# A scan one chunk ahead, a late operand, two gather buffers: one change to a layer with 32 experts on one core

## The chip, the cores and the metric

The kernel runs on one core of one Trainium2 chip. The metric is device time in microseconds, of one launch that computes the whole layer. The core has a matrix engine (PE, with its weight loads shown apart as PEld), a vector engine (DVE), an activation engine (ACT), GpSimd (POOL), a sync engine (SP) that mostly starts transfers, and 16 DMA engines. Each engine works through its own list of instructions in order and waits on semaphores.

## What is computed

The reference is one layer with 1024 tokens of width 1024, in float32:

```python
# mixing: three head groups side by side, then one output projection
h = rms_norm(x, norm_mix_g) * (1 + scale1) + shift1
p = h @ w_in                          # split into the inputs of the three groups
y = concat(ssd_mixer(...),            # 512 wide: scan over chunks of 128 tokens
           forgetting_attention(...), # 256 wide
           conformer_conv(...))       # 256 wide
x = x + gate * (y @ w_out)
# experts: 4 groups of 8, top-1 group, top-2 experts in it
h = rms_norm(x) * (1 + scale2) + shift2
weights = top_p / sum(top_p) * p_group
x = x + gate2 * sum_k weights_k * expert_k(h)
expert(h) = (silu(h @ w_gate) * (h @ w_up)) @ w_down      # 1024 -> 512 -> 1024, 32 experts
out = rms_norm(x) * g
```

(The block is shortened; names of small parameters are left out.) The scan of one chunk needs the state that the chunk before it left.

## The kernel before

The 1024 tokens lie in 8 blocks of 128. Float32 products are made of three matmuls: each operand is split into a high part, which ACT casts, and a low part, which DVE or POOL subtracts (the helper `split`, lines 127 and 128), and high by high, low by high and high by low are added in PSUM.

The kernel is written against a planner. It takes every operation with its dependences and due times and fixes the order of the instructions on each engine; at run time an engine keeps to that order. What is written as a loop with generators (`next(ssd)`, `next(post)`) therefore says which pieces of work lie near each other, and the planner decides the rest. `issue_after`, `add_manual_dep` and `after_load` bind an instruction behind another; the depth given to `after_load` (DC for the first NC_ loads of expert weights, DEPTH later, DL at the end) says how many loads back it is bound.

The stages that matter here:

- **Ahead of the output projection.** `others()` runs the input projections, and in their shade the attention's and convolution's norms (`att_norm`, lines 628 to 644) and `load_wo` (lines 806 to 822): 16 loads of raw weights `wr` through a pool of three buffers by SP, a product with the gate on DVE (816, 818), a cast on ACT and a subtract on DVE or POOL. In this stage the scan's first NSSD = 2 chunks run (`ssd_steps`, lines 680 to 765). A chunk's result is `yn`, written by L755.
- **Output projection**, one block after the other, 48 matmuls in 16 steps each (`c_steps`, L990 to L992). The order KORD takes the attention and convolution part of the operand first, and the scan's part from the fifth step of each half on. `c_pre` makes the operand `yh`, `yl`, both parts, at step CP = 11 of the block before: the attention and convolution part with casts and POOL subtracts, the scan part with four PE transposes of `yn` (L960), a cast and a subtract. Beside the steps of block b runs chunk b + 2 of the scan (blocks 0 to 5 have one), and the `post_steps` of block b - 1: transposes, router matmuls (L1016), logits (L1021, L1022), the second norm's h2 (L1025 and L1028; in the last block L1011, L1031 on ACT and L1032 on POOL), and its store to h2_d (L1033, on ACT's queue, in the last block on SP's).
- **Routing.** `route_steps` (lines 1054 to 1171) runs over batches of blocks, RB: blocks 0 to 3 after block 3, 4 to 6 after block 6, block 7 after block 7. It ranks the logits (L1076 to L1100), counts (L1109, L1112), and builds two tables by matmuls: tokens of each expert (L1130, added at L1134, cast to integers at L1138) and their weights (L1166, L1171).
- **Weights of the experts.** 192 loads of 1 MB, two to a matrix, in a ring of NHALF = 19 places ("halves") in tiles whose earlier content is dead: `room` and `room_of` hand out such a place and issue its first load when the place is free. Three of the places (w1, w2) come from the scan's pool, which is closed at block 6, where `xg` is also allocated and cleared; one is made of two small tiles (xqs[0] and "wg"). The last POST = 3 places are loaded behind the first gather.
- **Experts.** For each expert e an indirect DMA on POOL gathers its 128 rows of h2 into `xg` (`gather`, L1306); eight transposes (`xpose`, L1316) turn them; `next_tokens` makes the transposes of e and issues gather e + 1 at once behind them, into the same buffer. Weights are split by `piece` (L1326: a cast on ACT, a subtract on DVE), multiplied (L1338 to L1340, then L1366 to L1368) and the result is added to x1 in memory by an indirect DMA (L1376). After the last expert a tail norms and writes the output; it gathers x1's rows of the last expert into `xg`.

Of the kernel before, what the change touches and what calls it, by code (L numbers as in the profile page):

```python
# [30 lines left out]
NOV = 15  # L31
NSSD = 2
NHALF = 19
SB = 3
# [7 lines left out]
POST = 3  # L42
CP = 11
AN = 4
QD = 1
DC, NC_ = 2, 12
KORD = (4, 5, 6, 7, 0, 1, 2, 3)
# [5 lines left out]

RB = {3: (0, 4), 6: (4, 7), 7: (7, 8)}

# [19 lines left out]
def mixer_moe(ctx, tc, x, pch, prow, ada_m, ada_r, w_col, w_z, w_v, w_dtf, w_out, w_rt, w_gu, w_dn, out):  # L75
# [747 lines left out]
    def others():  # L823
# [11 lines left out]
        ats.enter_context(tc.tile_pool(name="pad", bufs=1)).tile([P, PAD], F32, name="pad")  # L835
        rawp = ats.enter_context(tc.tile_pool(name="wrp", bufs=3, reuse_waits="tile"))
        woc.update(rawp=rawp, hi=[wo.tile([P, KT, 512], F32R, tag=f"wo_hi{i}", name=f"wo_hi{i}") for i in range(2)],
# [114 lines left out]

    def c_pre(b, yn):
        bs = slice(b * P, (b + 1) * P)
        yh, yl = (yp.tile([P, 2, 4, P], F32R, tag=t, name=t) for t in ("yh", "yl"))
        split(yh[:, 1, 0:2], yl[:, 1, 0:2], cy[:, b, 2:4], G)
        split(yh[:, 1, 2:4], yl[:, 1, 2:4], cy[:, b, 0:2], G)
        pt = bank("ps_yt")
        for t in range(4):
            PE.transpose(pt[:, t * P:(t + 1) * P], yn[:, t], ident)  # L960
        split(yh[:, 0], yl[:, 0], pt.rearrange("p (t l) -> p t l", l=P))
        return yh, yl

# [14 lines left out]
    def c_steps(b, yh, yl, xbs):  # L978
        bs = slice(b * P, (b + 1) * P)
        xb = xin[b]  # L980
        xT = sc3.tile([P, KT, P], F32, tag="xT", name="xT")
        s2 = sc.tile([P, 4], F32, tag="s2", name="s2")
        h2 = sc3.tile([P, D], F32, tag="h2", name="h2")
        for q in range(2):
            qs_ = slice(512 * q, 512 * (q + 1))
            ps = bank("ps_wo", "pj")
            for n, kt in enumerate(KORD):
                hi, lo = (woc[k][q][:, kt] for k in ("hi", "lo"))
                h_, l_ = (y[:, kt // 4, kt % 4] for y in (yh, yl))
                PE.matmul(ps, h_, hi, start=(n == 0), stop=False)  # L990
                PE.matmul(ps, l_, hi, start=False, stop=False)
                PE.matmul(ps, h_, lo, start=False, stop=(n == KT - 1))  # L992
                if q and n == 5:
                    turn(xb, xT, 0)
                yield
            V.tensor_tensor(xb[:, qs_], ps, xb[:, qs_], op=ALU.add)
            S.activation(ps, xb[:, qs_], AF.Square, accum_out=s2[:, q:q + 1])
        s1 = S.dma_start(x1_d[bs, :], xb)
        if b == XB:
            room(xsp.tile([P, 4096], F32, name="w0"), s1.ins)  # L1000
            room_of(xqs[0], woc["gmp"].tile([P, D], F32, tag="gm", name="wg"), after=s1.ins)
            room_of(xqs[1], xqs[2], xqs_both, after=s1.ins)
        xbs.append((xb, xT, s2, h2))

    def post_steps(b, xb, xT, s2, h2):
# [23 lines left out]
        else:  # L1029
            with tc.issue_after(rc.ins):  # L1030
                S.mul(h2, h2, s2[:, 3:4])  # L1031
            G.tensor_tensor(h2, h2, ccn["shf"], op=ALU.add)  # L1032
        (S if b < NB - 1 else nc.sync).dma_start(h2_d[bs, :], h2)  # L1033
        if b + 2 < NB:
# [185 lines left out]
    load_x1(1, nc.sync)  # L1220
    nxt = c_pre(0, yns[0])
    post = iter(())
    ews = ExitStack()
    ew = None
    for b in range(NB):
        c = b + NSSD
        ssd = ssd_steps(c, yns, **cst) if c < NB else iter(())
        if c >= NB and ew is None:
# [3 lines left out]
            room(ew.tile([P, 2048], F32, name="w2"))  # L1232
            xg = ew.tile([P, D], F32, name="xg")
            G.memset(xg, 0.0)
        yh, yl = nxt
        for n, _ in enumerate(c_steps(b, yh, yl, xbs)):
# [4 lines left out]
            if b == 2 and n == 15:  # L1241
                run_all(an)
            if n == CP and b + 1 < NB:
                nxt = c_pre(b + 1, yns[b + 1])
                if b + 1 == 3 or b + 1 == 7:
                    room(cy[:, b - 2:b + 2].rearrange("p b c l -> p (b c l)"))
            if b == NB - 1 and n == 0:
# [56 lines left out]
    with tc.tile_pool(name="ex", bufs=2, reuse_waits="tile") as ex:  # L1304
        def gather(e):
            return G.indirect_dma_start(xg[:, :], None, h2_d[:, :],  # L1306
                                 bass.IndirectOffsetOnAxis(ap=toki[:, e:e + 1], axis=0),
                                 bounds_check=T - 1, oob_is_err=False)

        def xpose(e):  # L1310
            xh = ex.tile([P, KT, P], F32R, tag="xh", name="xh", bufs=1)
            xl = ex.tile([P, KT, P], F32R, tag="xl", name="xl", bufs=1)
            for q in range(2):
                pt = bank("ps_xg")
                for j in range(4):
                    PE.transpose(pt[:, j * P:(j + 1) * P], xg[:, (4 * q + j) * P:(4 * q + j + 1) * P], ident)  # L1316
                split(xh[:, 4 * q:4 * q + 4], xl[:, 4 * q:4 * q + 4], pt.rearrange("p (j c) -> p j c", c=P))
# [63 lines left out]
        with tc.issue_after(g1.ins):  # L1381
            for h in halves[NHALF - POST:]:
                G.memset(h[0][:, 0:1], 0.0)
        for _ in range(POST):
            load_half()
# [13 lines left out]
        def next_tokens(e):  # L1399
            if e < NE:  # L1400
                xt.append(xpose(e))
                if e + 1 < NE:
                    gather(e + 1)

# [37 lines left out]
        for b in LORD:  # L1442
            nc.sync.dma_start(xbs[b], x1_d[b * P:(b + 1) * P, :])
        xr, XE = xg, G
        rows_of = bass.IndirectOffsetOnAxis(ap=toki[:, NE - 1:NE], axis=0)
# [190 lines left out]
```

## Time and profile before

| | us |
|---|---|
| median of three timed runs | 1296.21 |
| lowest and highest | 1293.31, 1296.91 |
| the profiled execution | 1301.8 |
| its span, first to last instruction | 1299.9 |
| mean granted TensorE clock in it | 0.968 |
| PE busy | 1202.9 |
| DVE busy | 976.7 |
| ACT busy | 738.4 |
| POOL busy | 270.6 |

All rows below are of this one profiled execution, in microseconds from its start. A row of an engine's timeline has the start, the duration, the engine, the line, the operation, the output and inputs with their shapes, how many instructions were put together, and in brackets how long the engine had been idle before it and what released it ("issue" is none of the things that the profile shows). SPq and ACTq are those engines' sequencers, where transfers are issued. [...]

### The profile page before, as it was taken

The numbers are of one execution on the slowest core, as the hardware profiler recorded it, in microseconds if no ns is written. First come the engines' busy times: TensorE is split into PE (matmuls) and PEld (weight loads), VectorE is DVE, ScalarE is ACT, GpSimd is POOL, SyncE is SP. The second block draws the span as 40 slices with busy tenths as digits, with TensorE's granted clock in tenths as the row PEclk, the third lists the DMA queues.
The fourth block names the chain that finished last, engine by engine and source line by source line (L and its number), as shares of the span: only waits on it lengthen the run. The fifth ranks groups of instructions, "written<-read, shape, count | busy, mean of one in ns | idle before, by whom it ended". The sixth has DMA issues, their size and how long they took to land. (4 is left out here: it accounts for less than half of the span.)

```text
span 1299.9 us, 17279 instructions
## 1 busy us (share of the span) xinstructions
PE 1202.9 (93%) x6079; PEld 930.8 (72%) x6079; DVE 976.7 (75%) x1384; ACT 738.4 (57%) x1146; POOL 270.6 (21%) x200
## 2 busy tenths in 40 slices
PE   5999989999999879999789899999999999999993
PEld 4676646867677558778577677778777877787772
DVE  4789961145265676565678888999999999999985
ACT  4323312233354656653257676777777777787763
POOL 3110302300100253432112222221222122211113
PEclk9999989999999979999879999999999999999997
DMA  9315658642301453734979999999999999999726
GB/s 360 131 42 162 205 166 270 165 114 68 110 17 45 138 171 98 272 109 171 363 267 328 322 321 336 329 364 366 362 359 368 358 364 363 370 359 377 244 53 251
DMA packets 94635, 313.21 MB, mean 241 GB/s; under 512 B 24038, under 2 KB 34454, under 8 KB 73424
## 3 DMA queue, kind: packets, MB, share of 16 engines
q1 hardware_dynamic: 62190, 256.77, 54.3%
q10 hardware_dynamic: 14098, 31.99, 7.2%
q0 software_dynamic: 18256, 23.30, 7.2%
q8 instruction: 49, 0.80, 0.2%
q14 instruction: 42, 0.34, 0.1%
HBM read 289.22 MB, written 39.88 MB: 253 GB/s over the span
## 5 line engine op out<-in xcount | busy, mean ns | idle before, releaser
L1340 PE MATMUL ps_gu<-plo,xh 128*128 128x512 f32 x512 | 209.8, 410 | 7.9 <-DVE plo L1326 7.9
L1338 PE MATMUL ps_gu<-phi,xh 128*128 128x512 f32 x512 | 204.6, 400 | 0.0
L1339 PE MATMUL ps_gu<-phi,xl 128*128 128x512 f32 x512 | 201.8, 394 | 0.6 <-DVE xl L128 0.6
L1326 ACT CAST phi<-wx 128x1024 fp32r<-128x1024 f32 x160 | 167.4, 1053 | 61.6 <-PE ps_gu L1339 55.1
L1326 DVE TENSOR_TENSOR plo<-wx,phi 128x1024 fp32r<-128x1024 f32 x160 | 191.4, 1221 | 14.1 <-ACT phi L1326 9.9
L1376 POOL DMA_INDIRECT x_d<-early,toki x31 | 76.2, 2457 | 378.8 <-DVE early L1372 374.7
L1326 DVE TENSOR_TENSOR plo<-w,phi 128x1024 fp32r<-128x1024 f32 x104 | 125.2, 1221 | 10.8 <-ACT phi L1326 7.9
L1326 ACT CAST phi<-w 128x1024 fp32r<-128x1024 f32 x104 | 108.6, 1052 | 37.3 <-PE ps_gu L1339 32.9
L1340 PEld LDWEIGHTS ps_gu<-plo,xh 128*128 128x128 f32 x512 | 97.1, 190 | 38.0 <-DVE plo L1326 18.5
L1339 PEld LDWEIGHTS ps_gu<-phi,xl 128*128 128x128 f32 x512 | 97.3, 190 | 21.1 <-DVE xl L128 1.4
L1338 PEld LDWEIGHTS ps_gu<-phi,xh 128*128 128x128 f32 x512 | 97.2, 190 | 18.9 <-ACT xh L127 0.4
L1366 PE MATMUL ps_d<-phi,hh 128*128 128x512 f32 x256 | 100.8, 395 | 0.7 <-ACT hh L127 0.7
L1367 PE MATMUL ps_d<-phi,hl 128*128 128x512 f32 x256 | 100.4, 392 | 0.0
L1368 PE MATMUL ps_d<-plo,hh 128*128 128x512 f32 x256 | 96.6, 392 | 0.0
L182 PE MATMUL ps_pr<-h_hi,whi 128*128 128x512 f32 x224 | 91.7, 409 | 0.0
L184 PE MATMUL ps_pr<-h_hi,wlo 128*128 128x512 f32 x224 | 89.2, 398 | 1.3 <-POOL wlo L128 1.3
L183 PE MATMUL ps_pr<-h_lo,whi 128*128 128x512 f32 x224 | 89.3, 398 | 0.0
L223 DVE SCALAR_TENSOR_TENSOR cy<-u_t,cmw,cy 128x1024 f32<-128x1024 f32 x60 | 86.8, 1446 | 2.3 <-ACT cy L220 1.4
L128 POOL TENSOR_TENSOR wlo<-wraw,whi 128x1024 fp32r<-128x1024 f32 x14 | 38.3, 2748 | 178.8 <-ACT whi L127 124.6
L1306 POOL DMA_INDIRECT xg<-h_d,toki x32 | 38.6, 1208 | 109.1 <-PE ps_xg L1316 94.3
L990 PE MATMUL ps_wo<-wo_hi,yh 128*128 128x512 f32 x128 | 55.0, 432 | 1.5 <-ACT yh L127 1.5
L1366 PEld LDWEIGHTS ps_d<-phi,hh 128*128 128x128 f32 x256 | 48.3, 189 | 10.8 <-ACT hh L127 0.9
(403 smaller groups left out, 2629.4 us busy)
## 6 DMA issues: line engine op xcount, KB each, us to landing
wx<-in_w_gu_dram SPq DMA_DIRECT2D x53, 1024.0 KB, 11.6
w<-in_w_gu_dram SPq DMA_DIRECT2D x31, 1024.0 KB, 9.9
wx<-in_w_dn_dram SPq DMA_DIRECT2D x24, 1024.0 KB, 11.7
w<-in_w_dn_dram SPq DMA_DIRECT2D x19, 1024.0 KB, 10.9
at<-in_ada_r_dram ACTq DMA_DIRECT2D x64, 256.0 KB, 4.8
cy<-in_w_gu_dram SPq DMA_DIRECT2D x14, 1024.0 KB, 5.3
wy<-in_w_gu_dram SPq DMA_DIRECT2D x28, 512.0 KB, 13.8
wraw<-in_w_col_dram SPq DMA_DIRECT2D x16, 512.0 KB, 6.0
```

The lines of the kernel that those rows point to most:

```text
L182: PE.matmul(ps, hi[:, kt, :], h_hi[hf][:, kt, :], start=(kt == 0), stop=False)
L183: PE.matmul(ps, hi[:, kt, :], h_lo[hf][:, kt, :], start=False, stop=False)
L184: PE.matmul(ps, lo[:, kt, :], h_hi[hf][:, kt, :], start=False, stop=(kt == KT - 1))
L223: yield lambda t=t, k=k: V.scalar_tensor_tensor(cy[:, :, t], v128(u_t[:, t, k:k + T]), cmw[:, t, k:k + 1], cy[:, :, t], op0=ALU.mult, op1= ...
L1326: last[:] = [S.copy(hi, raw).ins, V.tensor_tensor(lo, raw, hi.bitcast(F32), op=ALU.subtract).ins]
L1338: PE.matmul(ps, xh[:, kt], hi[:, ks], start=(kt == 0), stop=False)
L1339: PE.matmul(ps, xl[:, kt], hi[:, ks], start=False, stop=False)
L1340: PE.matmul(ps, xh[:, kt], lo[:, ks], start=False, stop=(kt == KT - 1))
L1366: PE.matmul(pd[n], hh[:, f], hi[:, ns], start=(f == 0), stop=False)
L1367: PE.matmul(pd[n], hl[:, f], hi[:, ns], start=False, stop=False)
L1368: PE.matmul(pd[n], hh[:, f], lo[:, ns], start=False, stop=(f == 3))
L1376: G.indirect_dma_start(x1_d[:, :], bass.IndirectOffsetOnAxis(ap=toki[:, e:e + 1], axis=0), yo[:, :], None, bounds_check=T - 1, oob_is_err= ...
```

## The change

The scan starts with one chunk ahead instead of two, so that beside block b runs chunk b + 1, and blocks 0 to 6 have one. `c_pre` makes only the attention and convolution part of the operand, as before in the block before; a new `c_pre_scan` makes the scan's part in the block itself, at step CS = 1. The scan's pool is closed at block 7. The raw output weights have six buffers. There are two gather buffers, the second in xqs[0]; the ring of weights has 18 places, and the first 15 loads have depth DC. Routing's batches are 0 to 3, 4 and 5, 6 and 7. In the last block h2 is made by one DVE instruction, and its store is issued by ACT. Gather 1 is issued behind gather 0 and the clearing of the last three places; gather e + 2 behind the transposes of e.

```diff
-NSSD = 2
-NHALF = 19
+NSSD = 1
+NHALF = 18
...
+CS = 1
...
-DC, NC_ = 2, 12
+DC, NC_ = 2, 15
...
-RB = {3: (0, 4), 6: (4, 7), 7: (7, 8)}
+RB = {3: (0, 4), 5: (4, 6), 7: (6, 8)}
...
-        rawp = ats.enter_context(tc.tile_pool(name="wrp", bufs=3, reuse_waits="tile"))
+        rawp = ats.enter_context(tc.tile_pool(name="wrp", bufs=6, reuse_waits="tile"))
...
-    def c_pre(b, yn):
-        bs = slice(b * P, (b + 1) * P)
+    def c_pre(b):
         yh, yl = (yp.tile([P, 2, 4, P], F32R, tag=t, name=t) for t in ("yh", "yl"))
         split(yh[:, 1, 0:2], yl[:, 1, 0:2], cy[:, b, 2:4], G)
         split(yh[:, 1, 2:4], yl[:, 1, 2:4], cy[:, b, 0:2], G)
+        return yh, yl
+
+
+    def c_pre_scan(yn, yh, yl):
         pt = bank("ps_yt")
         for t in range(4):
             PE.transpose(pt[:, t * P:(t + 1) * P], yn[:, t], ident)
         split(yh[:, 0], yl[:, 0], pt.rearrange("p (t l) -> p t l", l=P))
-        return yh, yl
...
-            room_of(xqs[0], woc["gmp"].tile([P, D], F32, tag="gm", name="wg"), after=s1.ins)
...
-            with tc.issue_after(rc.ins):
-                S.mul(h2, h2, s2[:, 3:4])
-            G.tensor_tensor(h2, h2, ccn["shf"], op=ALU.add)
-        (S if b < NB - 1 else nc.sync).dma_start(h2_d[bs, :], h2)
+            V.scalar_tensor_tensor(h2, h2, s2[:, 3:4], ccn["shf"], op0=ALU.mult, op1=ALU.add)
+        S.dma_start(h2_d[bs, :], h2)
...
-            xg = ew.tile([P, D], F32, name="xg")
-            G.memset(xg, 0.0)
+            xgs = [ew.tile([P, D], F32, name="xg"), xqs[0]]
+            for xg in xgs:
+                G.memset(xg, 0.0)
...
+            if n == CS:
+                c_pre_scan(yns[b], yh, yl)
             if n == CP and b + 1 < NB:
-                nxt = c_pre(b + 1, yns[b + 1])
-                if b + 1 == 3 or b + 1 == 7:
-                    room(cy[:, b - 2:b + 2].rearrange("p b c l -> p (b c l)"))
+                nxt = c_pre(b + 1)
+            if b == 2 and n == CP or b == 7 and n == CS:
+                o = 0 if b == 2 else 4
+                room(cy[:, o:o + 4].rearrange("p b c l -> p (b c l)"))
...
-            return G.indirect_dma_start(xg[:, :], None, h2_d[:, :],
+            return G.indirect_dma_start(xgs[e % 2][:, :], None, h2_d[:, :],
...
+        gather(1)
         for _ in range(POST):
             load_half()
...
-                if e + 1 < NE:
-                    gather(e + 1)
+                if e + 2 < NE:
+                    gather(e + 2)
...
-        xr, XE = xg, G
+        xr, XE = xgs[0], G
```

## Rows read from the trace of the kernel before

**Rows 1.** The page: busy time of the engines, share of the span, instructions.

```profile
PE 1202.9 (93%) x6079; PEld 930.8 (72%) x6079; DVE 976.7 (75%) x1384; ACT 738.4 (57%) x1146; POOL 270.6 (21%) x200
```

**Rows 2.** Windows of the second half: from and to, length, then busy time and instructions of PE, PEld, DVE, ACT and POOL, granted clock, DMA share, GB/s.

```profile
650.00:660.00 10.00, 7.73 (x33) 7.04 (x33) 6.74 (x22) 3.33 (x5) 1.35 (x4) 0.50 0.40 141
...
700.00:800.00 100.00, 90.76 (x423) 74.19 (x422) 88.86 (x90) 71.80 (x80) 21.16 (x10) 0.98 0.93 327
800.00:900.00 100.00, 98.30 (x450) 79.45 (x449) 92.62 (x94) 75.66 (x85) 18.54 (x11) 0.98 0.96 341
900.00:1000.00 100.00, 98.35 (x456) 79.65 (x455) 96.27 (x99) 77.96 (x89) 17.27 (x10) 1.00 0.99 368
...
1200.00:1260.00 60.00, 59.19 (x274) 47.09 (x273) 56.78 (x59) 45.61 (x53) 10.70 (x6) 1.00 0.52 159
```

**Rows 3.** PE's timeline, transposes of gathered rows that waited, experts 0 to 8.

```profile
698.92 0.30 PE L1316 MATMUL ps_xg<-ident,xg 128*128 128x128 f32 x1 [2.92 <-DMA xg<-h_d,toki]
...
720.06 0.41 PE L1316 MATMUL ps_xg<-ident,xg 128*128 128x128 f32 x2 [3.26 <-DMA xg<-h_d,toki]
...
739.35 0.52 PE L1316 MATMUL ps_xg<-ident,xg 128*128 128x128 f32 x3 [1.36 <-DMA xg<-h_d,toki]
...
759.24 1.08 PE L1316 MATMUL ps_xg<-ident,xg 128*128 128x128 f32 x4 [1.99 <-DMA xg<-h_d,toki]
...
799.20 0.85 PE L1316 MATMUL ps_xg<-ident,xg 128*128 128x128 f32 x6 [2.63 <-DMA xg<-h_d,toki]
```

**Rows 4.** PE's timeline, the first gate matmul of experts 1, 8 and 9.

```profile
675.32 0.50 PE L1338 MATMUL ps_gu<-phi,xh 128*128 128x512 f32 x1
...
815.80 0.39 PE L1338 MATMUL ps_gu<-phi,xh 128*128 128x512 f32 x1
...
834.27 0.39 PE L1338 MATMUL ps_gu<-phi,xh 128*128 128x512 f32 x1
```

**Rows 5.** Windows cut where DVE adds the second half of a block (L996): the stretch ahead of the output projection, one block with a chunk of the scan, the two blocks without, and the stretch to the first expert. Columns as in rows 2.

```profile
434.00:467.30 33.30, 22.91 (x126) 15.25 (x125) 25.22 (x43) 24.50 (x72) 15.15 (x12) 0.80 0.52 150
...
541.80:562.60 20.80, 20.02 (x117) 16.38 (x117) 11.45 (x21) 12.83 (x44) 7.75 (x8) 1.00 0.58 200
...
606.10:620.30 14.20, 14.20 (x77) 10.61 (x77) 4.96 (x10) 3.99 (x10) 3.79 (x4) 1.00 0.96 364
620.30:635.10 14.80, 14.02 (x73) 10.05 (x72) 9.85 (x43) 2.52 (x7) 2.35 (x2) 1.00 0.91 339
635.10:658.40 23.30, 12.88 (x68) 10.69 (x69) 16.43 (x67) 7.19 (x12) 5.11 (x6) 0.60 0.71 271
```

**Rows 6.** The timeline of all engines around the start of the output projection.

```profile
454.62 10.50 SPq L814 DMA_DIRECT2D wr<-in_w_out_dram  x5
...
461.30 2.08 PE L625 MATMUL ps_crs<-ident,crs 128*128 128x128 f32 x8 [4.53 <-POOL crs L124]
...
463.42 0.75 DVE L644 SCALAR_TENSOR_TENSOR cy<-cy,early,ps_crs 128x512 f32<-128x512 f32 x1 [3.04 <-PE ps_crs L625]
...
467.35 0.73 PE L990 MATMUL ps_wo<-wo_hi,yh 128*128 128x512 f32 x2 [1.47 <-ACT yh L127]
```

**Rows 7.** The timeline at three places where the scan's operand is made: a subtract of DVE, a chunk's result, and the first matmul of the block that follows it.

```profile
518.76 0.69 DVE L128 TENSOR_TENSOR yl<-ps_yt,yh 128x512 fp32r<-128x512 f32 x1 [2.56 <-ACT yh L127]
...
559.65 0.62 DVE L755 TENSOR_SCALAR yn<-yy,ssr 128x256 f32<-128x256 f32 x2 [0.82 <-POOL ssr L124]
...
562.35 0.40 PE L990 MATMUL ps_wo<-wo_hi,yh 128*128 128x512 f32 x1
```

**Rows 8.** The timeline of all engines between the last block and the first expert, and one earlier instruction, L1025 of block 6.

```profile
622.82 1.28 DVE L1025 SCALAR_TENSOR_TENSOR h<-xb,s,af 128x1024 f32<-128x1024 f32 x1 [0.67 <-POOL s L124]
...
637.90 0.43 PE L1016 MATMUL ps_rt<-xT,wrp 128*64 128x128 f32 x2
...
638.91 2.02 PE L1166 MATMUL ps_tab<-roh,rph 128*128 128x32 f32 x12 [0.58 <-DVE tab L1134]
...
640.87 1.12 PE L1016 MATMUL ps_rt<-xT,wrp 128*64 128x128 f32 x8
...
642.99 0.26 DVE L1021 SCALAR_TENSOR_TENSOR L<-ps_rt,s,rbias 128x36 f32<-128x36 f32 x1 [1.83 <-PE ps_rt L1020]
...
643.50 2.34 POOL L1032 TENSOR_TENSOR h<-h,shf 128x1024 f32<-128x1024 f32 x1 [4.33 <-ACT h L1031]
...
643.76 2.10 DVE L1077 TENSOR_TENSOR rc<-L,rm 128x4 f32<-128x4 f32 x1
...
645.87 0.33 SPq L1033 DMA_DIRECT2D h_d<-h  x1
...
647.14 0.17 DVE L1077 TENSOR_TENSOR rc<-rel,rm 128x8 f32<-128x8 f32 x1
...
652.37 0.40 PE L1130 MATMUL ps_tab<-rEv,rph 128*128 128x32 f32 x1 [0.48 <-DVE jcol L1388]
```

**Rows 9.** The timeline of POOL and PE: the issue of gather 0, the transposes that waited for it, and the issue of the gather that rows 3 show waited for first.

```profile
653.95 1.17 POOL L1306 DMA_INDIRECT xg<-h_d,toki  x1 [8.11 <-DVE toki L1138]
...
658.40 1.97 PE L1316 MATMUL ps_xg<-ident,xg 128*128 128x128 f32 x8 [0.59 <-DMA xg<-h_d,toki]
...
689.90 1.99 POOL L1306 DMA_INDIRECT xg<-h_d,toki  x1 [13.25 <-PE ps_xg L1316]
```

**Rows 10.** The last loads of expert weights (SP's timeline), the last casts of them for gate and up (ACT's), and a line of the page's list of DMA issues (count, size, us to landing).

```profile
1219.92 6.43 SPq L1197 DMA_DIRECT2D w<-in_w_dn_dram  x4
...
1258.52 1.05 ACT L1326 CAST phi<-w 128x1024 fp32r<-128x1024 f32 x1 [0.77 <-PE ps_gu L1339]
...
wx<-in_w_dn_dram SPq DMA_DIRECT2D x24, 1024.0 KB, 11.7
```

More of the change, by code (lines that the diff above doesn't have):

```diff
@@ L1220, in mixer_moe @@
     load_x1(1, nc.sync)
-    nxt = c_pre(0, yns[0])
+    nxt = c_pre(0)
     post = iter(())
@@ L1315, in xpose @@
                 for j in range(4):
-                    PE.transpose(pt[:, j * P:(j + 1) * P], xg[:, (4 * q + j) * P:(4 * q + j + 1) * P], ident)
+                    PE.transpose(pt[:, j * P:(j + 1) * P], xgs[e % 2][:, (4 * q + j) * P:(4 * q + j + 1) * P], ident)
                 split(xh[:, 4 * q:4 * q + 4], xl[:, 4 * q:4 * q + 4], pt.rearrange("p (j c) -> p j c", c=P))
```

## The prediction, made before the result

> **What bounds the kernel now.** I began with the page's busy shares [rows 1]: PE works 93% of the span, so an edit pays only where PE waits now, or where it takes work off the path between two PE stages. [...] PE's own timeline names the loss [rows 3]: five of the first eight experts stop in the middle of the matmuls, at transposes L1316, because the gather of the next expert's rows hasn't landed. The first gate matmul of experts 1, 8 and 9 [rows 4] gives its full size: one steady expert takes 834.27 - 815.80 = 18.47 us, seven took 815.80 - 675.32 = 140.48, and 7 x 18.47 = 129.29, so 11.2 us are lost. The waits of rows 3 sum to 2.92 + 3.26 + 1.36 + 1.99 + 2.63 = 12.16, which is the same loss seen from the other side. With one buffer the gather of e+1 can only start when the transposes of e are through, and it needs longer than the planner left for it.
>
> For the middle of the kernel I read windows cut at the ends of the output projection's blocks [rows 5]. A block with scan work takes 20.8 us with PE busy 20.02; blocks without take 14.2 and 14.8. So these blocks are PE-bound, and one chunk of scan in a block costs 20.8 - 14.5 = 6.3 us. The stretch ahead (434 to 467.3) has PE busy 22.91 of 33.3 at clock 0.80, and the stretch behind (635.1 to 658.4) 12.88 of 23.3 at 0.60. Those two are bound by chains of small steps [rows 6, 8], not by PE.
>
> **Two gather buffers.** Added: one more memset of the buffer (POOL, inside block 7, beside 14 us of PE work) and one gather ahead of the loop. Gather e+2 is issued where gather e+1 was, so each has a whole further expert (18.5 us) to land; the loaded gather issued at 689.90 was landed at 698.92, after 9.0 us [rows 3, 9]. That removes the waits: -11.2. Bounds: -12.2 if all of rows 3 goes, -7 if the DMA queue or the weights take back two of the five waits (about 2.1 each). What is late next is the weights, which pay with one ring place (19 halves to 18; a half is 1 MB, 3.1 us at the 341 GB/s of 800 to 900, near the 327 of 700 to 800). The last weight load is issued at 1219.92, the last gate or up cast that uses weights starts at about 1258 [rows 10]; with some 12 us of flight (11.7 in the page's list of issues) that leaves a cushion of about 26 us (an estimate from those rows). Spent of it are 11.2 + 3.1 and what the transition saves. It stays positive, and 0.07 of DMA time stands open between 700 and 800 [rows 2]. So 0 for the lost half.
>
> **The transition from the last block to expert 0** [rows 8, 9]. (a) The batches {4-5} and {6-7} replace {4-6} and {7}. Now twelve L1166 matmuls of the middle batch stand between the two groups of the last block's router matmuls: the first group ends at 638.33, the second starts at 640.87. In the new order that batch is done a block earlier: -2.5, and -0.2 for the table matmuls ahead of the first group. (b) The last batch has two blocks. Each further block adds two L1130 of 0.40 and wider DVE steps: +1.0 (0.5 to 2). (c) The last h2 was an ACT multiply and a POOL add of 2.34; while POOL ran, a 4-element DVE subtract (L1077) took 2.10, and the same line takes 0.17 at 647.14. With no POOL pass beside it that is -1.9. (d) The new fused DVE instruction takes what L1025 took, 1.28, on the DVE that runs the chain to the token table: +0.6, half of it, because DVE has a gap of 1.83 us ahead of L1021; 0 if it goes there, 1.28 if it goes in front of the router's steps. (e) The store moves from SP to ACT. Its issue is 0.33 us, it went out at 645.87, eight microseconds ahead of the gather, so 0 either way; ACT waits for the DVE step with only the router's small exponent pass and weight casts behind it: 0, or the 1.28 of (d) a second time if that pass is held. SP no longer holds the following loads behind a wait. (f) Rooms open a block later (the scan's pool closes at block 7, not 6), so some three loads are still in flight when gather 0 is issued. Alone it landed in 4.4 us (653.95 to 658.35), loaded in 9.0: +2 between 0 and +4.6, nearer to the unloaded row since only the tail of the loads overlaps it. Sum: -2.7 + 1.0 - 1.9 + 0.6 + 2 = **-1.0** (from -4.1 to +3.3).
>
> [...] The rows say 4.4 us alone and 9.0 beside weights [rows 3, 9]. [...]
>
> **Out-projection.** Chunk 1 leaves the stretch ahead of it and runs in block 0. (a) Start: the first L990 waits for yh of the attention part, which hangs on L644 and L625, and L625 waited 4.53 for POOL's crs [rows 6]. Chunk 1's instructions stand in PE's, DVE's and ACT's queues between these. If the chain alone sets the start, 0; if all of chunk 1's PE work lay in front, 6.3/0.80 = -7.8. I take -5, nearer to the second, since PE, ACT and DVE are each busy for two thirds or more of that stretch [rows 5]. (b) Chunk 1's PE work comes back in block 0 where it doesn't find gaps: 0 to +6.3; +3, because part of chunk 1 already ran behind the first L990 and the clock there is low. Chunk 2 moves to block 1 and so on: seven blocks at 20.8 and one at 14.5 stand against six and two with a longer block 0, which is the same PE work. (c) Six buffers for the raw weights: SP stood 10.50 us in five of these loads [rows 6], waiting for buffers, with the constants for block 0 queued behind. -2 (0 to -4). (d) The scan operand is made last. Its four transposes at step 1 need yn of the previous block's scan, and then an ACT cast and a DVE subtract ahead of step 4. Now yn is ready at 560.27 and the next block's L990 start at 562.35 [rows 7], 2.1 us of margin, with one to two matmul steps on top. The cast can sit behind ACT's scan work: at 518.76 DVE waited 2.56 for it. I take 0, since the transposes have matmuls of the attention part behind and before them as cover; +2 per block if that is gone. Sum: -5 + 3 - 2 = **-4** (from -11.8 to +8, one late block counted).
>
> **The sum**: -11.2 - 1.0 - 4 = -16.2. The profiled execution took 1301.8; 1285.6 would be its successor. It stands 5.6 above the median of 1296.2, which I carry over: **1280**.
>
> **Rivals.**
> A. The out-projection starts with the whole -7.8 and finds gaps for chunk 1 (0 in place of +3), and gather 0 meets no load: another 8 us, 1272. For it: PE idles 10.4 of 33.3 us in that stretch. Against: the clock is 0.80 there and the attention chain keeps its length.
> B. The second buffer doesn't do what it says: the planner puts the transposes of e+1 earlier into expert e (they need only the buffer), or POOL issues the gather behind the scatter L1376 that waits for early. Then the early experts still lose, and only the other terms, -5, remain: 1291. For it: L1316 stands well ahead of its expert even now [rows 3]. Against: a gather has 18 us more.
> C. The weights are late: prefetch begins a block later and the ring is shorter, so that the cushion is used up and the experts follow the DMA at 0.99 share [rows 2]. Half of the 11.2 would stay with the DMA, and about 2 with the transition: 1288. Against it: 26 us of cushion and 0.52 share at the end.
> D. Slower than before: the scan operand is late in every block. PE, in order, stops at the transposes for yn, or at step 4 for yh behind ACT's rh/rl and square passes. With margin 2.1 plus 0.7 to 1.4 us of steps it begins when yn comes more than about 3 us later within its block than now. It decides the sign from 16.2/8 = 2.0 us a block; at 3.2, a bit above the wait of rows 7 (2.56), 25.6 go against 16.2: 1280 + 25.6 = 1306. For it: the wait in rows 7, and that the scan now has one block instead of two. Against: yn ends before its block's end in rows 7.
>
> **Chances and range.** Forecast 0.62, A 0.13, B 0.09, C 0.06, D 0.10. From the bounds of the terms, the forecast case alone runs from 1268 (all terms at their low ends, -28.1) to 1300 (all at their high ends, +4.3); the high end needs several misses at once, so I take half of that way, 1290. The range 1266 to 1293 takes in A's, B's and C's centres and leaves out D and the ends of A. About 0.3% (3.9 us) is what a measurement of this kernel can tell: faster is below 1292.3, slower above 1300.1. Faster: 0.62 + 0.13 + 0.04 of B + 0.05 of C = 0.84, less 0.02 for the forecast's tail = 0.82; same 0.08; slower 0.10.
>
> **What would show it.** Right: no PE wait on a gather at L1316 after expert 0; experts 1 to 8 at about 18.5 us each; no 12 matmuls between the two router groups; L1077 at 0.17 in the last block; from last block's end to the first transposes about 22 us; first L990 some 5 us earlier. Wrong: L1316 still waiting for DMA (B); ACT casts waiting for DMA weights after 800 us (C); PE waiting for yn or yh at the scan transposes or at step 4 in each block (D).

## The result and the profile after

| | before | changed |
|---|---|---|
| median | 1296.56 | 1304.74 |
| lowest, highest | 1293.31, 1298.67 | 1302.32, 1304.79 |
| span of the profiled execution | 1299.9 | 1300.5 |

The ratio is 1.0055, with a 95% interval from 1.0031 to 1.0079: slower by some 7 to 8 us, where 1280 was forecast. One launch of a later kernel, after_nc12, took 4093.7 us and is left out of its ratio. The two profiled executions hide the difference: that of before (1301.8) is slower than every other execution of its kernel here, that of the changed kernel the fastest of its four (1302.32). In them the stages moved so (ends read from the same instructions):

| stage | before | changed | difference | forecast |
|---|---|---|---|---|
| first matmul of the output projection | 467.35 | 473.39 | +6.0 | -5 and -2 |
| from it to the last block's end (DVE L996, now L999) | 167.8 | 170.7 | +3.0 | +3 |
| from there to expert 0's first gate matmul | 25.1 | 32.5 | +7.5 | -1.0 |
| expert 0 to expert 31, first gate matmuls (the last at 1240.45 and 1241.74) | 580.3 | 565.1 | -15.2 | -11.2 |

So the experts gave all that was promised, and more, and the front and the transition took it back. That the blocks came out at the forecast +3 is luck, as the section after the experiments shows.

Windows of the changed kernel, with the columns of [rows 2]: the stretch ahead of the output projection, a block with scan work, the one block without, the transition, and two stretches of experts.

```profile
434.00:473.39 39.39, 17.41 (x76) 12.59 (x77) 32.13 (x46) 20.52 (x55) 18.96 (x17) 0.61 0.54 157
...
540.82:561.32 20.50, 19.84 (x116) 16.18 (x115) 11.56 (x21) 12.75 (x42) 7.88 (x8) 1.00 0.44 140
...
628.56:644.12 15.56, 15.52 (x91) 12.11 (x90) 5.83 (x18) 3.85 (x9) 2.34 (x2) 1.00 0.90 337
644.12:674.61 30.49, 10.05 (x54) 8.59 (x54) 14.64 (x58) 5.29 (x9) 3.99 (x6) 0.62 0.94 350
700.00:800.00 100.00, 99.55 (x471) 81.75 (x470) 97.52 (x100) 80.03 (x90) 23.04 (x11) 1.00 0.98 361
900.00:1000.00 100.00, 98.32 (x456) 79.68 (x455) 96.24 (x98) 78.15 (x90) 17.25 (x10) 1.00 0.99 364
```

Against [rows 2, 5]: 700 to 800 went from 90.76 to 99.55 of PE. The stretch ahead of the output projection is longer although PE has less to do in it (17.41 against 22.91), and DVE more (32.13 against 25.22); PE is idle for 22.0 us of it, before for 10.4. The mean granted clock over it, a share of full speed, fell from 0.80 to 0.61: it stood at 0.50 from 443 to the end, some 30 us, where before had it there for some 14 (442 to 445 and 455.5 to 465.7). The transition has PE busy 10.05 of 30.49.

PE's waits in the expert stage of the changed kernel (what was waited for: us in all, times, longest):

```profile
PE ps_gu L1344 <- DVE plo L1330: 8.9, 27, 0.4
PE ps_gu L1342 <- ACT xh L128: 1.4, 1, 1.4
```

These are all of them from 676 to 1260 us. No gather is left; the five stops of [rows 3] are gone. The transition shows where time went instead. First the router's chain on PE, DVE and POOL, then SP, then PE again:

```profile
645.45 1.40 PE L1018 MATMUL ps_rt<-xT,wrp 128*64 128x128 f32 x16
...
649.52 0.17 DVE L1077 TENSOR_TENSOR rc<-L,rm 128x8 f32<-128x8 f32 x1
...
659.27 1.17 POOL L1310 DMA_INDIRECT xg<-h_d,toki  x1 [11.76 <-DVE toki L1138]
```

```profile
653.33 7.17 SPq L1197 DMA_DIRECT2D wx<-in_w_gu_dram  x3
...
665.20 0.33 SPq L1197 DMA_DIRECT2D wx<-in_w_dn_dram  x1
665.58 0.32 SPq L1278 DMA_DIRECT2D sl<-g_rows  x1
...
670.93 3.75 PE L1284 MATMUL ps_row<-sl,ident 8*128 8x128 f32 x16 [11.30 <-DMA sl<-g_rows]
674.61 1.97 PE L1320 MATMUL ps_xg<-ident,xg 128*128 128x128 f32 x8
...
676.65 0.78 PE L1342 MATMUL ps_gu<-phi,xh 128*128 128x512 f32 x1
```

The chain to gather 0 is shorter, as forecast: the two router groups are one run of 16, L1077 takes 0.17, and the gather is issued 659.27 - 644.12 = 15.2 us after the last block's end, against 18.8 [rows 5, 9]. But the gather isn't what PE waits for. `sl` is a load of eight rows, the gate of the second sub-layer; 16 small matmuls (L1284, L1280 before) spread it over the partitions, and expert 0 needs it only for its result. In PE's list they stand ahead of expert 0's transposes, and in SP's list the load stands behind the weight loads of block 7. The longest of SP's waits from 600 to 680 say what held it:

```profile
SPq L1197 <- DVE cy L756: 21.0, 1, 21.0
SPq L1197 <- DMA w<-in_w_gu_dram: 11.5, 3, 4.7
SPq L1197 <- DMA wx<-in_w_gu_dram: 10.8, 3, 4.7
SPq L1197 <- DMA wx<-in_w_dn_dram: 8.2, 3, 3.3
SPq L1197 <- DMA cy<-in_w_dn_dram: 5.4, 1, 5.4
```

First a room that the last chunk of the scan opens a block later: SP waited about as long for it before (23.6), but that wait ended at 605.73, and this one at 626.23. Then one load after the other that may not start before the load two ahead of it has landed. Before, `sl` went out at 646.25, right behind the store of [rows 8], 11.1 us after the last block's end; now at 665.58, 21.5 us after it, and PE began with it 5.3 us later.

At the front, DVE, PE and PE again, around the last piece of attention:

```profile
463.72 0.28 DVE L594 COPY ph<-ps_pt 128x128 f32<-128x128 f32 x1
...
464.06 0.69 PE L598 MATMUL ps_o<-ph,vst 128*64 128x128 f32 x2 [5.67 <-DVE ph L594]
...
473.39 1.22 PE L993 MATMUL ps_wo<-wo_hi,yh 128*128 128x512 f32 x2 [1.94 <-ACT yh L128]
```

### The profile page after: what moved, and what is told of

It reads as the page before. It is cut to its first block, busy times and chain, and to the rows that moved or that the text cites. A ratio compares the mean times of both kernels' runs of the same rounds, so it can differ in the third digit from the quotient of the medians.

```text
span 1300.5 us, 17257 instructions
## 1 busy us (share of the span) xinstructions
PE 1194.5 (92%) x6079; PEld 928.8 (71%) x6079; DVE 978.4 (75%) x1386; ACT 737.8 (57%) x1145; POOL 264.1 (20%) x200
## 5 line engine op out<-in xcount | busy, mean ns | idle before, releaser
L1330 DVE TENSOR_TENSOR plo<-wx,phi 128x1024 fp32r<-128x1024 f32 x166 | 198.0, 1220 | 7.9 <-ACT phi L1330 5.2
L1330 ACT CAST phi<-wx 128x1024 fp32r<-128x1024 f32 x166 | 173.1, 1055 | 50.8 <-PE ps_gu L1343 41.8
L1330 ACT CAST phi<-w 128x1024 fp32r<-128x1024 f32 x110 | 115.4, 1050 | 59.0 <-PE ps_gu L1343 50.9
L1330 DVE TENSOR_TENSOR plo<-w,phi 128x1024 fp32r<-128x1024 f32 x110 | 130.7, 1220 | 6.8 <-ACT phi L1330 5.5
L1330 DVE TENSOR_TENSOR plo<-cy,phi 128x1024 fp32r<-128x1024 f32 x44 | 53.7, 1221 | 3.5 <-ACT phi L1330 1.6
```

The costliest lines, as they stand in the source:

```text
L1330: last[:] = [S.copy(hi, raw).ins, V.tensor_tensor(lo, raw, hi.bitcast(F32), op=ALU.subtract).ins]
```

## The experiments

Ratios are to the kernel before, on the same chip, with 95% intervals. The runs were made in three sets on three chips, in which the kernel before had medians of 1296.52, 1295.07 and 1296.93; the changed kernel itself was timed only for the result, four times. A difference to it is one of medians, and the ratios beside it say how far it can be trusted. Theory 1 after reading the trace: the gathers are cured; the six buffers or the scan's place delay the front; `sl` delays the transition.

**sl_act.** The changed kernel and

```diff
     def row_load(src, dst):
-        nc.sync.dma_start(dst, src.rearrange("(a b) -> a b", b=P))
+        S.dma_start(dst, src.rearrange("(a b) -> a b", b=P))
```

> The changed kernel with one edit: the small load of eight rows (sl) that PE's 16 broadcast matmuls wait for before expert 0 is issued by ACT instead of SP. Theory 1 (in the changed kernel that load is queued on SP behind weight loads that are held, and PE's in-order list puts the first expert's transposes behind its matmuls): the first expert starts when gather 0 has landed, 8 to 11 us earlier, 1294 to 1297 us. Rival (gather 0 itself, or the first weights, are as late as sl): first expert starts no more than 2 us earlier, 1302 to 1305 us.

`row_load` has a second caller, a small row for the last norm that SP issued at 604.81, ahead of the long wait; it moves to ACT too. 1298.21, ratio 1.0019 (1.0004 to 1.0035), 6.5 us less than the changed kernel by the medians and 4.7 by the ratios. The first gate matmul came 23.5 us after the last block, not 32.5. The PE rows of this kernel:

```profile
660.15 3.78 PE L1284 MATMUL ps_row<-sl,ident 8*128 8x128 f32 x16
...
666.47 1.94 PE L1320 MATMUL ps_xg<-ident,xg 128*128 128x128 f32 x8 [2.55 <-DMA xg<-h_d,toki]
```

The wait on `sl` is gone and the next one shows, on gather 0 beside weight loads, issued at 659.85 and 6.6 us on its way. The transition is 9.0 us shorter, as theory 1 says (8 to 11), but the time is just above its range: 2.6 us go again in the experts, 567.7 from expert 0 to 31 in place of 565.1, since fewer of the early ones run fast (last section).

**back_only** and **two_gather**, on the kernel before. The second has the lines of the diff that speak of `xgs`, `xqs`, `gather` and NHALF; the first adds

```diff
-RB = {3: (0, 4), 6: (4, 7), 7: (7, 8)}
+RB = {3: (0, 4), 5: (4, 6), 7: (6, 8)}
-DC, NC_ = 2, 12
+DC, NC_ = 2, 15
...
+            V.scalar_tensor_tensor(h2, h2, s2[:, 3:4], ccn["shf"], op0=ALU.mult, op1=ALU.add)
+        S.dma_start(h2_d[bs, :], h2)
```

> The kernel before with the back half of the change alone: two gather buffers and 18 ring places, the batches 4-5 and 6-7, h2 of the last block by one DVE instruction and its store by ACT, 15 loads with the small depth. The scan stays two chunks ahead, three buffers for raw output weights. Theory 1: the output projection ends as before (635), the gathers' waits go (-15 in the expert stage) and the chain to the token table is 3.7 shorter; rooms open a block earlier than in the changed kernel, so sl is held little: 1277 to 1283 us. Rival (the back half by itself holds sl behind weight loads, because its loads go two at a time): expert 0 some 8 to 11 later than that, 1286 to 1293 us.

> The kernel before with the two gather buffers and 18 ring places alone. Theory 1: only the expert stage changes, by -11 to -15: 1281 to 1285 us. Rival (the lost ring place, or weight loads that run two at a time behind the second gather, take the gain back): expert stage ends up waiting for weights, 1289 to 1296 us.

1288.18 (0.9935, 0.9912 to 0.9958) and 1288.66 (0.9933, 0.9912 to 0.9954). Both gain 8 us, less than theory 1 had for either, and the edits of the transition (batches, h2 and its store, depth) add nothing to it. PE's waits for weights are as in the changed kernel (8.7 and 8.9 us), so two_gather's rival isn't what took the rest. In two_gather PE has a new wait in front of expert 0:

```profile
655.21 1.97 PE L1316 MATMUL ps_xg<-ident,xg 128*128 128x128 f32 x8 [0.43 <-DMA xg<-h_d,toki]
...
662.26 0.45 PE L1316 MATMUL ps_xg<-ident,xq 128*128 128x128 f32 x1 [5.08 <-DMA xq<-h_d,toki]
662.36 0.78 PE L1338 MATMUL ps_gu<-phi,xh 128*128 128x512 f32 x1
```

xq is the second buffer. With a second gather in flight the planner puts the first of expert 1's transposes ahead of expert 0's first matmul, and PE waits there for gather 1 (theory 2). In back_only the gather is issued 3.6 us sooner after the last block (14.6 against 18.2), but `sl` and gather 1 are waited for (4.1 and 1.9 us). So its rival is there in part, and its time lies in the rival's range. From the last block's end to the first gate matmul it is 27.4 us against 29.6, but the blocks take 169.8 against 167.1: what left the transition came back in front of it.

**front_only.** The changed kernel with those back edits undone.

> The changed kernel with the back half undone: scan one chunk ahead, scan operand made last, six buffers for raw output weights, but one gather buffer, 19 ring places, the old batches, old h2 and store. Theory 1 (the front half makes the output projection end 9 us later by itself): 1303 to 1308 us, last block's end near 644. Rival (the late end comes from the back half's batches and loads in the blocks): last block's end near 635, 1295 to 1299 us.

1313.41 (1.0130, 1.0107 to 1.0152), worse than any theory had it. In its profiled execution, the slowest of six (1318.78), the last block ends at 643.54, as theory 1 says. Another 10 us are in the transition (35.3 against 25.1), since the last store of h2 is on SP here, behind the held loads, and gather 0 waits for it (SP, then POOL):

```profile
655.66 0.58 SPq L1036 DMA_DIRECT2D h_d<-h  x1
...
672.57 1.50 POOL L1312 DMA_INDIRECT xg<-h_d,toki  x1 [19.28 <-DMA h_d<-h]
```

The two halves sum: +16.9 and -8.3 make +8.6, the whole change has +8.2. Their terms don't sum, though: this front pays for the store on SP, the whole change for `sl`.

**after_wrp3** and **before_wrp6** part the front's two suspects.

```diff
-        rawp = ats.enter_context(tc.tile_pool(name="wrp", bufs=6, reuse_waits="tile"))
+        rawp = ats.enter_context(tc.tile_pool(name="wrp", bufs=3, reuse_waits="tile"))
```

> The changed kernel with three buffers for the raw output weights again, all else as changed. Theory 1 (six buffers let the planner put the products and splits of the output weights on DVE, ACT and POOL ahead of the last attention steps, so the first matmul of the output projection starts 6 to 8 us later): first L993 near 465 instead of 473 to 475, 1295 to 1299 us. Rival (one chunk ahead instead of two is what delays the start, since PE has less to do and falls to the low clock): start and time as in the changed kernel, 1303 to 1306 us.

> The kernel before with six buffers for the raw output weights alone. Theory 1: the first output matmul starts 6 to 8 us later, 1302 to 1306 us. Rival (the number of buffers is harmless, one chunk ahead is the cause): 1294 to 1298 us.

1296.44 (1.0011, 0.9994 to 1.0027), 8.3 less than the changed kernel by the medians and 5.7 by the ratios, and 1302.86 (1.0064, 1.0042 to 1.0085), 7.8 more than the kernel before in the runs beside it. The six buffers alone make the start late, whichever way the scan runs: by 7.3 us with one chunk ahead, by 12 with two. In before_wrp6 the blocks, 160.2 us long, win most of that back, and the last one ends 4.3 us late. That fits its profiled execution (1299.96, 4.9 above the median of before beside it and among the faster of its eleven); what the slower ones, up to 1309.0, had more stands in no trace. DVE's last attention copy and PE's first output matmul, in after_wrp3 and then in before_wrp6:

```profile
450.90 0.28 DVE L594 COPY ph<-ps_pt 128x128 f32<-128x128 f32 x1
...
466.06 1.22 PE L993 MATMUL ps_wo<-wo_hi,yh 128*128 128x512 f32 x2 [2.54 <-ACT yh L128]
```

```profile
463.55 0.28 DVE L593 COPY ph<-ps_pt 128x128 f32<-128x128 f32 x1
...
479.22 0.58 PE L990 MATMUL ps_wo<-wo_hi,yh 128*128 128x512 f32 x1
```

The order that the planner wrote says the same. The number of DVE's instructions in the trace, up to and with that copy, is

```
three buffers: 464, scan one (after_wrp3) or two (before) chunks ahead
six buffers:   477, scan one (changed) or two (before_wrp6) chunks ahead
```

DVE's busy time up to there is 260.6 and 260.3 us with three buffers, 274.2 and 274.2 with six: 13 instructions and 14 us more in front of the copy. With buffers free, 14 of the 16 raw loads are out by 448 in the changed kernel (9 by 452 before), and the planner puts their products and subtracts, 0.7 us and more each on DVE, ahead of the copy on which the attention part of the operand hangs.

**two_gather_late1.** Theory 2 on two_gather: expert 1's transposes are bound behind the first gate matmuls.

```diff
+                    with tc.issue_after(gl[0]) if e == 1 else nullcontext():
                         PE.transpose(pt[:, j * P:(j + 1) * P], xgs[e % 2][:, ...
```

(`gl[0]` is the last gate matmul made so far.)

> Two gather buffers and 18 ring places on the kernel before, and the transposes of expert 1 bound behind the first gate matmuls of expert 0. In the run without that binding PE waited 5.08 us for gather 1 at those transposes, ahead of the first gate matmul. Theory 2 (with a second gather in flight the planner puts its transposes ahead of expert 0, and part of the gain goes into that wait): about 5 us faster than two gather buffers alone, 1282 to 1285 us. Rival (expert 0 waits for something else at that place, such as its weights, or the early experts give it back to the weights): 1287 to 1290 us.

1284.82 (0.9908, 0.9882 to 0.9933): 3.8 us less than two_gather by the medians, 3.2 by the ratios, whose intervals overlap. The trace decides: the first gate matmul follows gather 0's transposes at once.

```profile
654.89 1.97 PE L1317 MATMUL ps_xg<-ident,xg 128*128 128x128 f32 x8 [0.57 <-DMA xg<-h_d,toki]
...
656.69 0.80 PE L1339 MATMUL ps_gu<-phi,xh 128*128 128x512 f32 x1
```

From the last block to it are 24.6 us, not 29.6, and the experts give 1.8 of the 5.0 back (567.6 against 565.8 from 0 to 31). Theory 2 holds.

**back_sl_late1**: back_only with both mends.

> The back half of the change on the front of the kernel before, with the small load sl issued by ACT and the transposes of expert 1 bound behind expert 0's gate. Theories 1 and 2 together: expert 0 starts when gather 0 has landed, some 6 us earlier than with the back half alone (1288): 1280 to 1284 us. Rival (the early start is given back to the weights, whose cushion is gone): 1286 to 1289 us.

1284.65 (0.9916, 0.9894 to 0.9938), the same as two_gather_late1 and slower than expected. Gather 0 is issued 14.6 us after the last block, 3.7 sooner than there, but needs 8.7 us where it needed 4.4 there, and the gain goes into PE's wait for it:

```profile
656.20 1.94 PE L1315 MATMUL ps_xg<-ident,xg 128*128 128x128 f32 x8 [4.08 <-DMA xg<-h_d,toki]
```

**best_nc12** and **after_nc12** put 12 of the loads at the small depth again, on back_sl_late1 and on the changed kernel.

```diff
-DC, NC_ = 2, 15
+DC, NC_ = 2, 12
```

> The back half of the change on the front of the kernel before, with sl issued by ACT, the transposes of expert 1 bound behind expert 0's gate, and only the first 12 loads at the small depth as before. With 15 of them gather 0 took 8.7 us from issue to its transposes, beside weight loads that SP had been held back with; with 12, in the two-buffer kernel, 4.4. Theory 3 (15 loads two at a time only push loads back into the gather's way): gather 0 lands 4 us earlier, 1279 to 1282 us. Rival (more loads at once make the gather or the first weights later): 1284 to 1288 us.

> The changed kernel with 12 in place of 15 loads at the small depth, nothing else. Theory 3: SP is held less ahead of sl, which goes out earlier; first expert 3 to 8 us earlier, 1297 to 1302 us. Rival (SP is held by rooms that open late, not by the depth): 1303 to 1306 us.

best_nc12: 1282.82 (0.9893, 0.9874 to 0.9912), the fastest of all, 1.8 us below back_sl_late1 by the medians, which the intervals can't part. The time is 0.8 above the expected range. The mechanism is as expected, gather 0 lands 5.2 us after its issue, and from the last block to the first gate matmul it is 21.7 us instead of 25.0:

```profile
650.44 1.17 POOL L1304 DMA_INDIRECT xg<-h_d,toki  x1 [11.32 <-DMA wx<-in_w_gu_dram]
...
655.68 1.94 PE L1315 MATMUL ps_xg<-ident,xg 128*128 128x128 f32 x8 [0.74 <-DMA xg<-h_d,toki]
```

after_nc12: 1300.12 (1.0030, 1.0015 to 1.0044), 4.6 less than the changed kernel by the medians, 3.2 by the ratios, whose intervals overlap. `sl` goes out at 655.62 in place of 665.58, and PE still waits 7.18 for it:

```profile
655.62 0.78 SPq L1278 DMA_DIRECT2D sl<-g_rows  x1
...
668.50 3.75 PE L1284 MATMUL ps_row<-sl,ident 8*128 8x128 f32 x16 [7.18 <-DMA sl<-g_rows]
```

The depth is a good part of what held SP.

**after_store_sp.**

```diff
-        S.dma_start(h2_d[bs, :], h2)
+        (S if b < NB - 1 else nc.sync).dma_start(h2_d[bs, :], h2)
```

> The changed kernel with the last store of h2 on SP again, nothing else. Theory 5 (the store then stands behind the same held weight loads as sl, and gather 0 waits for it): gather 0 is issued 6 to 10 us later, the first expert 2 to 6 us later, 1306 to 1311 us. The forecast's reading (the queue of the store is worth nothing): 1303 to 1306 us.

1309.92 (1.0106, 1.0085 to 1.0126), 5.2 more than the changed kernel. The store goes out at 662.77, not 648.86, and gather 0 waits 25.49 us on POOL for it:

```profile
662.77 0.42 SPq L1033 DMA_DIRECT2D h_d<-h  x1
...
672.66 1.47 POOL L1310 DMA_INDIRECT xg<-h_d,toki  x1 [25.49 <-DMA h_d<-h]
```

The gather is issued 13.4 us later, more than theory 5 had; its time is as expected, and theory 5 holds. The store's move to ACT is worth this where SP is held, that is, with the changed front.

**one_ahead_clean** has the changed front and best_nc12's back: after_wrp3 with sl by ACT, expert 1's transposes bound, 12 loads at the small depth.

> The changed kernel (one chunk ahead, operand made last) without what the other runs found to cost: three buffers for raw output weights, sl by ACT, transposes of expert 1 behind expert 0's gate, 12 loads at the small depth. Against the kernel that has the same back but the scan two chunks ahead it prices the scan's place alone. Theory 4 (the chunk fills gaps of PE ahead of the output projection when it is two ahead, and none in block 6): 3 to 5 us slower than that kernel, 1283 to 1287 us. Rival (the scan's place is free, as the forecast's sum had it): within 1 us of that kernel.

1291.54 (0.9963, 0.9949 to 0.9978), 8.7 above best_nc12, more than the 3 to 5 expected. It has the late operand as well as the scan's new place, so the 8.7 are of both; PE's waits for `yh` and `yl` in its blocks sum to 1.3. Block 6, which now has a chunk, and block 7, in one_ahead_clean and in best_nc12:

```profile
599.82:621.48 21.66, 19.41 (x111) 15.15 (x109) 16.58 (x54) 7.45 (x24) 6.14 (x7) 1.00 0.26 89
621.48:637.03 15.55, 15.51 (x91) 12.11 (x90) 5.83 (x18) 3.85 (x9) 2.34 (x2) 1.00 0.94 344
```

```profile
605.62:619.74 14.12, 13.95 (x73) 9.96 (x71) 9.37 (x45) 3.06 (x9) 3.77 (x4) 1.00 0.88 335
619.74:635.73 15.99, 15.96 (x93) 12.57 (x92) 5.82 (x17) 3.80 (x9) 2.34 (x2) 1.00 0.75 247
```

Block 6 costs 7.5 us more. All the blocks together take 172.7 us from the first output matmul to the last block's end, against 168.2: 4.5 of the 7.5 aren't won back in the others, of which block 0 wins most (30.8 against 34.7). And DMA, which could load weights at 335 GB/s in block 6, moves 89 there, because the rooms of the scan's pool open a block later. Those loads then run beside gather 0, which lands 9.2 us after its issue (652.17 to 661.34) instead of 5.2: the other 4 us. (In these two executions the output projection also starts at 464.34 against 467.58, within the spread of starts with three buffers, so the profiled times are only 6.3 apart.)

## Why the prediction was wrong

Two steps gave the sign: step (c) of the output projection took six buffers for a gain of 2 where they cost 6 to 8, and step (e) of the transition put the order of SP's list at nothing where the transition got 7.5 us longer. A third, (a) of the output projection, forecast a start 5 us earlier that no kernel with three buffers shows.

**Gathers, -11.2: right in mechanism, the size partly by luck.** -15.2 in the two profiles, and two things in it weren't forecast. The profiled execution of before had long gathers: before_wrp6, with the same gathers, waits 7.9 us for them where before waits 12.75 [rows 3, 9], and takes 575.7 us from expert 0 to 31, not 580.3. Against that one the gain is 10.6. And the forecast took 18.47 for every freed expert; the seven from 1 on take 125.67 in the changed kernel, not 129.29. Against a kernel before with shorter gathers the two errors nearly cancel. The lost ring place cost nothing, as forecast: no PE wait on a weight load. The new price that the forecast lacked is the wait for gather 1 ahead of expert 0, 5.08 us in two_gather; it asked of the added gather only when it would land, not where the planner would put the transposes that read it. In the changed kernel the wait for `sl` hides it.

**Transition, -1.0: the chain right, the sum wrong.** Steps (a) to (d), -3.0 together, measured -3.7 from the last block to the gather's issue. But step (a) counted as a gain what only moved: the middle batch now runs beside the blocks, which the prediction itself had called PE-bound. Block 7 takes 15.56 us with 91 matmuls where it took 14.80 with 73 [rows 5], and all the blocks are 1.0 to 2.6 us longer with the new batches than with the old (back_sl_late1 against two_gather_late1; back_only against two_gather and the changed kernel, 170.7, against front_only, 168.1). Step (e) failed: "SP no longer holds the following loads behind a wait" and "so 0 either way". It looked at the one store that leaves SP, and not at what stands on SP ahead of it and of `sl`. The weight loads wait themselves, for rooms and by their depth, and step (f), which did see that rooms open a block later, priced it only at the gather. So `sl` went out 10.3 us later after the last block, and the transition was 7.5 longer instead of 1.0 shorter; sl_act makes it 9.0 shorter again. The store's place was worth 5.2 (after_store_sp), not 0. Step (f)'s own size was right in sl_act: 6.6 us from issue to transposes, 2.2 above the 4.4 of [rows 9]. Those 4.4 weren't quite alone, as the prediction read them: the DMA share was 0.00 from the issue at 653.95 to 655.27, and then four weight loads came.

From issue to transposes gather 0 took 8.7 us in back_sl_late1, 9.2 in one_ahead_clean, 6.6 in sl_act and 5.2 in best_nc12. The DMA engines were 0.89 to 1.02 busy in all four, so their share alone doesn't tell which it will be. And 5.2 us hung on which engine issues the store (after_store_sp): SP works through its list in order, and the store stood there behind issues that waited, so that it went out at 662.77 and not at 648.86.

**Output projection, -4: two terms of three wrong.** (a), a start 5 us earlier because chunk 1 leaves the stretch: with three buffers the start is 466.06 and 464.34 with one chunk ahead, and between 464.87 and 467.58 in the kernels with two. That is the bound 0: the start comes as early with chunk 1 in the stretch as without it, so chunk 1 isn't what sets it. With six buffers one chunk ahead does start 5.8 us sooner than two (473.39 against 479.22 in before_wrp6), but still later than any start with three. (c), six buffers, -2: the sign was wrong, +5.7 and +8.3 by the ratios of the two pairs that change nothing else. It read SP's 10.50 us [rows 6] as time that others wait for; hardly anybody did (DVE 0.9 us in all ahead of the projection), and free buffers let the planner put the weights' work in front of attention's on DVE. (b), +3 for chunk 1's return, was of the right order, 4.5 in one_ahead_clean; that the table has +3.0 is luck, since 2.6 of it is the batches' (front_only, with the old ones, has 168.1), and six buffers shorten the blocks by themselves (160.2 in before_wrp6 against 167.8). (d), the late operand, cost nothing in the changed kernel: all of PE's waits from 476 to 644 are

```profile
PE ps_cb L706 <- DVE cbm L702: 2.1, 3, 0.8
PE ps_pos L1109 <- DVE rEv L1122: 1.5, 1, 1.5
PE ps_rt L1022 <- ACT rT L1020: 1.1, 3, 0.7
PE ps_pos L1109 <- DVE rohr L1103: 0.8, 1, 0.8
PE ps_tab L1130 <- DVE rph L1120: 0.6, 1, 0.6
```

with none for yn, yh or yl. So rival D didn't come about, and B only at one place, ahead of expert 0 (two_gather). C had the right seed (prefetch a block later) and the wrong victim, a small load and a gather in place of the experts' weights.

**The step to the median** failed too. 5.6 us were carried over as if a profiled execution lay above its median by a constant; that of before did so mostly by its own long gathers, and that of the changed kernel lies 2.4 below its median. So 8.0 of the 24.7 us between 1280 and 1304.74 are this step's, and 16.7 the stages'.

## What to carry to other kernels

Before giving an engine's queue more freedom or taking one instruction off it, list what stands ahead of and behind it in that queue, also the small transfers whose readers stand ahead of the important work on another engine. Give such loads a queue that nothing can hold. More buffers move work in a planned kernel, and where the planner puts it decides the sign; look at the written order before looking for time. Work that leaves a stage of waits for one that PE bounds isn't saved: count it where it lands.

## What the runs showed of the hardware that wasn't expected

The first experts that wait for no gather run faster than the late ones. In the changed kernel experts 1 to 5 take 17.64 to 17.82 us each, and PE is busy 99.55 of 100 us; from expert 6 on it is 18.46 each, and 98.32 of 100. Waits of 0.3 us for DVE's weight subtracts, 27 in all, make up part of the 0.7. How many experts run fast goes with the transition: five in each kernel with two buffers whose first gate matmul comes 27.4 us or more after the last block's end, three in each where it comes at most 26.1 after it. So some 2 us of a shorter transition are given back in the experts (2.6 in sl_act, 1.8 in two_gather_late1). Why the order settles into the slower pattern wasn't tried.
